# Loads, half scales and tied orders at the head of a two-layer trunk kernel

## The chip, the cores and the metric

The kernel runs on one core of one Trainium2 chip. The core has TensorE (PE in the profile: matrix products and transposes), VectorE (DVE), ScalarE (ACT), GpSimd (POOL) and SyncE (SP, which here issues nearly all transfers between memory and the on-chip buffers). Each engine works through its own list of instructions in order; an instruction waits where its inputs or its buffers are not ready. The metric is the device time of one execution in microseconds (us); the kernel before was timed three times.

## The reference

A sequence of 2048 rows of 1024 numbers goes through two layers, all in 32-bit floats. Only the first products of layer A matter here:

```python
def rms_norm(x, g):
    xf = x.astype(jnp.float32)
    y = xf * lax.rsqrt(jnp.mean(xf * xf, axis=-1, keepdims=True) + EPS)
    return (y * g.astype(jnp.float32)).astype(x.dtype)

def gmlp_mixer(h, w_in, ln_g, ln_b, w_s, b_s, w_out):
    u, v, z = jnp.split(h @ w_in, 3, axis=-1)
    ...

h = rms_norm(x, a_norm_g[i])
x = x + gmlp_mixer(h, a_w_in[i], ...)
```

Layer A normalises each row by its root mean square, scales it by a gain, multiplies by a 1024 x 6144 matrix, mixes in chunks, multiplies by an output matrix and adds. Layer B computes keys and values from the result, attends in bands of nine chunks of 64 rows, multiplies by an output matrix and adds; a last normalisation ends it.

## The kernel before

**Tiling.** The big products use a scheme of seven products in place of eight: rows and columns of the operands are cut in halves, and seven phases, numbered 1, 2, 6, 5, 7, 4, 3 in their order of time, multiply sums and differences of the quarters. The 2048 rows are 16 blocks of 128 rows, taken as eight pairs j = 0 to 7. The even block of a pair is loaded into a tile `ha`, the odd one ("second-row block") into `hb`; of `hb` there are three buffers. A quarter is 128 rows by 512 columns, the first or the second half of a block.

**Precision.** Each operand is a sum of two parts: a rounded one (`hi`, a CAST on ACT) and the difference (`lo`, a TENSOR_TENSOR on DVE). `split`, line 433, makes both. A product is three matrix products, `mm3`, lines 111 to 113: hi x hi, hi x lo of the weights, lo x hi. Lines 434 and 437 are therefore the roundings and the differences, of the weights (tiles `T`, `T_hh`, `T_hl`, 128 x 1024, from raw tiles `rw`) and of the left side (tiles `S`, 128 x 512).

**A block's way.** `block_norm`, line 692, makes four steps: `load` from `x` (line 697, and for block 0 also the gain `gab`), `square` on ACT (line 703), `power` (line 709, a small add on DVE into the tile `ra`, and line 710, the power -1/2 on POOL), `scale` on DVE (line 714), which multiplies the block by its factor and the gain. `s_split`, line 607, then transposes a quarter on PE in four products with the identity (line 611, into a tile `t`, of which there are four buffers), makes `S` hi and lo of it, and stores `S` to memory (`hsd`, line 614) for later passes. There are six `S` buffers. For each pair, `block_c` (line 728) also transposes the second half of `hb` for phase 4 and makes three sums on POOL (lines 734 to 736); `block_d` transposes the first half of `hb`, summed with the second, for phase 5.

**The first 16 steps.** A step is one phase and one pair. In the first 16 (phase 1, then phase 2, pairs 0 to 7 each) the same `S` is multiplied by two groups of weights, number 0 and number 1, 12 products each: 24 products of 128 x 512 per step. Weights of group 0 lie in `T` tiles (eight buffers), those of group 1 in a large tile, `T_hh` in phase 1 and `T_hl` in phase 2. `make_t`, line 448, gives each its `load`, `combine` and `finish` (the split).

**What sets the order.** `run_steps`, line 659, writes the program step by step: the events of a step, its products, then the preparation of the step three later (`LOOK = 3`), then the weights' functions due there. A planner then orders each engine's instructions by what it expects them to cost; a tie (`behind`, `in_order`) puts an instruction after another on its engine. Transfers go into SP's single list in that order. In the program before, the first two `ha` blocks are done by `first_two` (line 927), and ahead of everything PE multiplies zeros 32 times (line 879, tile `wp`).

Of the kernel before, what the change touches and what calls it, by code (L numbers as in the profile page):

```python
# [9 lines left out]
F32 = mybir.dt.float32  # L10
# [23 lines left out]
def trunk_kernel(  # L34
# [349 lines left out]
    with ExitStack() as actx:  # L384
# [43 lines left out]
        def paced(ins):  # L428

            if "evict" in last:  # L430
                behind(ins, last["evict"])

        def split(hi, lo, src, key=None):
            ins = nc.scalar.copy(hi, src)  # L434
            if key:
                in_order(key, ins)
            nc.vector.tensor_tensor(lo, src, hi.bitcast(F32), op=sub)  # L437
            return ins


# [166 lines left out]
        def s_split(ph, j, rows):  # L607

            pt = ptp[0].tile([P, 4, P], F32, tag="t0", name=f"t0_{ph}_{j}", bufs=4)
            for k in range(4):  # L610
                tpose(pt[:, k, :], rows[:, k * P : k * P + P], ident[:])
            t = s_tile(f"S0_{ph}_{j}")
            split(t[:, 0], t[:, 1], pt[:], "S")
            later(1, lambda: paced(nc.sync.dma_start(
                hsd[ph, j][:], t[:].rearrange("p a k c -> p a (k c)").bitcast(F32)
            )))
            return s_views(t)
# [41 lines left out]
        def run_steps(steps, ts, prep, act, events):  # L659


            left = {}
            for s in range(-LOOK, len(steps)):
                for f_ in events.get(s, []):
                    f_()
                if s >= 0:
                    act(s, *steps[s], left.pop(s))
                if s + LOOK < len(steps):
                    left[s + LOOK] = prep(*steps[s + LOOK])
                for f_ in ts.get(s, []):  # L670
                    f_()
# [20 lines left out]
        def block_norm(blk, t):  # L692
# [7 lines left out]

            def square():
                jk = ca.tile([P, D], BF16, tag="acc", name=f"jk{blk}", bufs=25)
                ins = nc.scalar.activation(
                    jk[:], t, AF.Square, scale=1.0 / 32, accum_out=r[:]
                )
                last["square"] = ins.ins.name

            def power():
                nc.vector.tensor_scalar(r[:], r[:], EPS, None, op0=add)
                ins = nc.gpsimd.tensor_tensor(r[:], r[:], mhalf[:], op=ALU.pow)  # L710
                last["power"] = ins.ins.name

            def scale():
                nc.vector.scalar_tensor_tensor(t, t, r[:], gab[:], op0=mul, op1=mul)
# [160 lines left out]
        wz = ca.tile([P, 512], F32R, tag="acc", name="wz", bufs=25)  # L875
        nc.gpsimd.memset(wz[:, 0:256].bitcast(F32), 0.0)
        wp = pmm.tile([P, 512], F32, tag="mm", name="wp")
        for i in range(32):
            mm(wp[:, 0:256], wz[:, 0:P], wz[:, 0:256], start=True, stop=True)
# [13 lines left out]
        for n in range(6):  # L893
            for ph in PH:
# [15 lines left out]
                    offs = ((-5, 1), (-4, 1), (-3, 1))  # L910
                if n == 5 and ph == 3:
                    where = in_big(n, ph, ("hl",))
                add_t(ts, s, n, ph, w_a[n], 2, where, chain_in(n, "hl" if n else "hh"), offs)

        def norm_at(load, s, block, j):
# [8 lines left out]
            ts.setdefault(s, []).append(lambda: todo.pop(0)())  # L924
            at(s + 1, lambda: todo.pop(0)())

        def first_two():
            for fs in zip(block_a(0), block_a(1)):
                for f_ in fs:
                    f_()  # L930
# [1084 lines left out]
```

## Time and profile before

| | |
|---|---|
| three runs | 2649.82, 2651.04, 2652.89 us; median 2651.04 |
| profiled execution | 2655.7 us, its span 2653.6 us |
| mean granted TensorE clock | 0.997 |
| busy in the span | PE 2607.4 us (98%), DVE 1894.2 (71%), ACT 1303.4 (49%), POOL 896.9 (34%) |
| transfers | 718.72 MB, mean 271 GB/s |

The profile is of one execution. Its times count from the span's start. In the rows of the timeline the columns are: start, length, engine, line of the kernel, operation, what it writes and reads, shape, and in brackets the idle time before it with what ended that. A row "x5" merges five that follow each other, and its length runs from the first's start to the last's end. SPq and POOLq are rows of an engine's issuing. Instructions on DVE and ACT overlap a little: the next starts some 0.1 us before the one ahead of it has ended. A row of waits gives the total, the count and the longest. A row of windows gives the stretch, its length, PE's busy time and count, the granted clock of PE (1.00 is full), the busy share of the transfer engines and GB/s.

### The profile page before, as it was taken

Reading aid. Unit: us, or ns where it says so; the run is one execution under the profiler, and the core shown is the slowest. Engines: PE = TensorE matmul, PEld = TensorE weight load, DVE = VectorE, ACT = ScalarE, POOL = GpSimd, SP = SyncE. Lnnn points to the kernel's source line nnn. Section 1 sums busy time; section 2 is a strip of 40 time slices with the busy share of each in tenths; the row PEclk is TensorE's granted clock in tenths of the full one; section 3 lists DMA queues with packets and bytes.
Section 4 is the critical chain, followed back from the end, with each engine's and each line's share of the span. In section 5 each row is a group of like instructions: output and inputs, shape, how many; then the busy total and the mean of one; then the engine's idle time right before and its main releaser. Section 6 shows DMA issues by size and latency. Waiting matters only on the chain. (4 is left out here: it accounts for less than half of the span.)

```text
span 2653.6 us, 37992 instructions
## 1 busy us (share of the span) xinstructions
PE 2607.4 (98%) x12960; PEld 2179.6 (82%) x12960; DVE 1894.2 (71%) x2944; ACT 1303.4 (49%) x2303; POOL 896.9 (34%) x874
## 2 busy tenths in 40 slices
PE   8999999999999999999999999999999999999998
PEld 7888888888888888888877778888887888888886
DVE  5655676866667667757776767778777777877677
ACT  5423243442433434343356466666656655665564
POOL 3611334143152422203234434344332232232245
PEclk9999999999999999999999999999999999999999
DMA  7899998989988869967775587778787666775667
GB/s 286 312 343 333 342 371 321 318 321 345 328 309 301 317 234 323 332 207 270 279 268 193 194 283 228 237 241 267 247 272 254 222 202 221 253 231 162 196 222 253
DMA packets 273856, 718.72 MB, mean 271 GB/s; under 512 B 28800, under 2 KB 68736, under 8 KB 273664
## 3 DMA queue, kind: packets, MB, share of 16 engines
q1 hardware_dynamic: 273664, 716.31, 78.5%
q8 instruction: 103, 1.69, 0.3%
q14 instruction: 89, 0.73, 0.1%
HBM read 531.12 MB, written 174.59 MB: 266 GB/s over the span
## 5 line engine op out<-in xcount | busy, mean ns | idle before, releaser
L111 PE MATMUL P<-T,S 128*128 128x512 f32 x1248 | 496.5, 398 | 2.1 <-ACT S L434 2.1
L112 PE MATMUL P<-T,S 128*128 128x512 f32 x1248 | 488.7, 392 | 0.6 <-DVE T L437 0.6
L113 PE MATMUL P<-T,S 128*128 128x512 f32 x1248 | 489.1, 392 | 0.0
L1437 POOL TENSOR_SCALAR pr<-pr,sl 128x640 f32<-128x640 f32 (+4 forms) x256 | 207.8, 812 | 549.2 <-DVE sl L1436 460.9
L111 PE MATMUL pj<-hh_b,wh_b 128*128 128x512 f32 x768 | 319.4, 416 | 0.9 <-ACT wh_b L228 0.9
L113 PE MATMUL pj<-hh_b,wl_b 128*128 128x512 f32 x768 | 303.9, 396 | 1.5 <-DVE wl_b L229 1.4
L112 PE MATMUL pj<-hl_b,wh_b 128*128 128x512 f32 x768 | 302.4, 394 | 0.1
L1433 ACT ACTIVATE pr<-pr,nm 128x640 f32<-128x640 f32 (+4 forms) x256 | 195.5, 764 | 186.9 <-DVE nm L1426 185.2
L113 PEld LDWEIGHTS P<-T,S 128*128 128x128 f32 x1248 | 235.2, 188 | 50.7
L111 PEld LDWEIGHTS P<-T,S 128*128 128x128 f32 x1248 | 235.6, 189 | 47.1 <-ACT S L434 2.3
L112 PEld LDWEIGHTS P<-T,S 128*128 128x128 f32 x1248 | 235.7, 189 | 45.6 <-DVE T L437 1.0
L1458 DVE TENSOR_TENSOR pt<-tp,pt 128x640 fp32r<-128x640 f32 (+4 forms) x256 | 188.5, 736 | 43.1 <-ACT pt L1457 40.5
L1426 DVE CUSTOM_DVE_ANT_0 pr<-s,bias 128x640 f32<-128x640 f32 (+4 forms) x256 | 188.0, 734 | 32.9 <-PE s L1418 27.0
L1457 ACT CAST pt<-tp 128x640 fp32r<-128x640 f32 (+4 forms) x256 | 158.9, 621 | 52.7 <-PE tp L1453 48.5
L1453 PE MATMUL tp<-ident,pr 128*128 128x128 f32 x1120 | 166.6, 275 | 9.7 <-DVE pt L1458 8.1
L113 PEld LDWEIGHTS pj<-hh_b,wl_b 128*128 128x128 f32 x768 | 144.1, 188 | 36.4 <-DVE wl_b L229 3.9
L1453 PEld LDWEIGHTS tp<-ident,pr 128*128 128x128 f32 x1120 | 130.5, 140 | 44.8 <-issue 16.1
L111 PEld LDWEIGHTS pj<-hh_b,wh_b 128*128 128x128 f32 x768 | 145.0, 189 | 19.0 <-ACT wh_b L228 2.6
L1478 PEld LDWEIGHTS pv<-pt,V 128*128 128x128 f32 x896 | 143.0, 188 | 20.6 <-DVE pt L1458 3.2
L112 PEld LDWEIGHTS pj<-hl_b,wh_b 128*128 128x128 f32 x768 | 145.1, 189 | 16.9 <-DVE hl_b L186 0.6
L1478 PE MATMUL pv<-pt,V 128*128 128x256 f32 (+3 forms) x896 | 154.0, 319 | 2.1 <-ACT pt L1457 1.1
L229 DVE TENSOR_TENSOR wl_b<-raw_b,wh_b 128x1024 fp32r<-128x1024 f32 x96 | 120.1, 1253 | 28.9 <-ACT wh_b L228 27.4
(302 smaller groups left out, 5737.4 us busy)
## 6 DMA issues: line engine op xcount, KB each, us to landing
S<-hsd SPq DMA_DIRECT2D x288, 512.0 KB, 5.5
rw<-in_w_a SPq DMA_DIRECT2D x108, 512.0 KB, 6.5
A<-ytd SPq DMA_DIRECT2D x72, 512.0 KB, 5.4
raw_b<-wk SPq DMA_DIRECT2D x72, 512.0 KB, 4.2
hsd<-S SPq DMA_DIRECT2D x56, 512.0 KB, 4.6
V<-vhd SPq DMA_DIRECT2D x56, 512.0 KB, 5.7
bias<-reld SPq DMA_DIRECT2D x64, 320.0 KB, 3.9
va<-vd SPq DMA_DIRECT2D x32, 512.0 KB, 6.5
```

What stands on the lines that cost most here:

```text
L111: first = mm(ps, lh, rh, start=first, stop=False)
L112: mm(ps, lh, rl, start=False, stop=False)
L113: mm(ps, ll, rh, start=False, stop=last)
L229: tv(wl[:], raw[:], wh[:].bitcast(F32), op=sub)
L1426: nc.vector.tensor_tensor_reduce(out=pr[:, c0:].rearrange("p (a b) -> p a b", a=nseg), in0=ps[:, :nseg, :w], in1=bias[:, c0:].rearrange("p ...
L1433: nc.scalar.activation(pr[:, c0:], pr[:, c0:], AF.Exp, scale=-1.0, bias=nm[:], accum_out=sl[:])
L1437: nc.gpsimd.tensor_scalar(pr[:, c0:], pr[:, c0:], sl[:], 1.0, op0=ALU.mult, op1=ALU.mult)
L1453: ins = tpose(tp[:, b, :], pr[:, b * P : (b + 1) * P], ident[:])
L1457: nc.scalar.copy(oh, tp[:, b0:5, :].rearrange("p a b -> p (a b)"))
L1458: nc.vector.tensor_tensor(pt[:, 2560 + o + b0 * P : 2560 + o + 640], tp[:, b0:5, :].rearrange("p a b -> p (a b)"), oh.bitcast(F32), op=ALU ...
L1478: mm(po[:, q0 * P : q1 * P], vtl[t, p][:, i, hs], rhs, start=(i == blocks[0] and j == 0), stop=(i == 7 and j == 1),)
```

## The change

Five things are done, all in the preparation of the first steps:

1. `opening` replaces `first_two`. Loads go in the order block 0, gain, both weights of group 0, block 1, both weights of group 1. Blocks 0 and 1 are scaled in halves of 512 columns: the first half of each, which phase 1 needs, early, the second halves at the end of the opening.
2. While `begin` is not empty, every instruction that goes through `first` is tied behind the one before it on ACT, and likewise on DVE.
3. 40 zero products instead of 32 come first, and eight more are tied behind block 0's transposes.
4. The weights of phase 2 for both groups are loaded from step 0 on (eight steps ahead of their phase), where they were loaded four to six steps ahead; the steps at which the program writes their split stay the same.
5. The second-row blocks 1 and 2 are loaded one and two steps earlier, that is before the first stores.

```diff
+        def first(eng, ins):
+            if begin:
+                in_order("first " + eng, ins)
+            return ins
...
             for k in range(4):
-                tpose(pt[:, k, :], rows[:, k * P : k * P + P], ident[:])
+                ins = tpose(pt[:, k, :], rows[:, k * P : k * P + P], ident[:])
+            last["tpose"] = ins.ins.name
...
+                if s == -LOOK:
+                    left.update(opening())
                 if s >= 0:
                     act(s, *steps[s], left.pop(s))
-                if s + LOOK < len(steps):
+                if s + LOOK < len(steps) and s + LOOK not in left:
...
-            def scale():
-                nc.vector.scalar_tensor_tensor(t, t, r[:], gab[:], op0=mul, op1=mul)
+            def scale(c=slice(0, D)):
+                first("dve", nc.vector.scalar_tensor_tensor(
+                    t[:, c], t[:, c], r[:], gab[:, c], op0=mul, op1=mul
+                ))
...
-        for i in range(32):
-            mm(wp[:, 0:256], wz[:, 0:P], wz[:, 0:256], start=True, stop=True)
+        def warm(n, after=None):
+            for i in range(n):
+                ins = mm(wp[:, 0:256], wz[:, 0:P], wz[:, 0:256], start=True, stop=True)
+                if after:
+                    behind(ins, after)
+
+        warm(40)
...
+                if n < 2 and ph == 1:
+                    continue
+                if n < 2 and ph == 2:
+                    offs = ((-8, 0), (-5 + n, 1), (-4 + n, 1))
...
-        at(-LOOK, first_two)
+        def opening():
+            begin.append(1)
...
+            load0()
+            for q in range(2):
+                l0(q)
+                c0(q)
+            load1()
+            for q in range(2):
+                l1(q)
+                c1(q)
+            square0()
+            power0()
+            scale0(h0)
+            f0(0)
+            views[0] = prep(*steps[0])
+            warm(8, last["tpose"])
+            f0(1)
+            square1()
+            f1(0)
+            power1()
+            scale1(h0)
+            f1(1)
+            views[1] = prep(*steps[1])
+            scale0(h1)
+            scale1(h1)
+            return views
+
+        at(0, begin.clear)
...
-            norm_at(e - 1, e, block_b, j)
+            norm_at((-1, -1, 0)[j] if j < 3 else e - 1, e, block_b, j)
```

DVE at the very start, rows of the program before (`ra` the factor of a block, `S_1_0` and `S_1_1` the left sides of steps 0 and 1, `T_1` the weights of phase 1, the last number a buffer's):

```order
L714 SCALAR_TENSOR_TENSOR ha_377<-ha_377,ra_378,gab 128x1024
L709 TENSOR_SCALAR ra_380<-ra_380 128x1
L714 SCALAR_TENSOR_TENSOR ha_379<-ha_379,ra_380,gab 128x1024
L437 TENSOR_TENSOR S_1_0_399<-t_1_0_394,S_1_0_399 128x512
L437 TENSOR_TENSOR T_1_01_407<-rw_1_000_402,T_1_00_406 128x1024
L437 TENSOR_TENSOR T_1_11_411<-rw_1_001_404,T_1_10_410 128x1024
L437 TENSOR_TENSOR T_1_hh<-rw_1_000_414,T_1_hh 128x1024
L437 TENSOR_TENSOR S_1_1_448<-t_1_1_443,S_1_1_448 128x512
L437 TENSOR_TENSOR T_1_hh<-rw_1_001_416,T_1_hh 128x1024
L709 TENSOR_SCALAR ra_422<-ra_422 128x1
```

and of the change:

```order
L724 SCALAR_TENSOR_TENSOR ha_385<-ha_385,ra_386,gab 128x512
L444 TENSOR_TENSOR T_1_01_406<-rw_1_000_391,T_1_00_405 128x1024
L444 TENSOR_TENSOR S_1_0_414<-t_1_0_409,S_1_0_414 128x512
L444 TENSOR_TENSOR T_1_11_426<-rw_1_001_393,T_1_10_425 128x1024
L444 TENSOR_TENSOR T_1_hh<-rw_1_000_396,T_1_hh 128x1024
L719 TENSOR_SCALAR ra_388<-ra_388 128x1
L724 SCALAR_TENSOR_TENSOR ha_387<-ha_387,ra_388,gab 128x512
L444 TENSOR_TENSOR T_1_hh<-rw_1_001_398,T_1_hh 128x1024
L444 TENSOR_TENSOR S_1_1_444<-t_1_1_439,S_1_1_444 128x512
L724 SCALAR_TENSOR_TENSOR ha_385<-ha_385,ra_386,gab 128x512
L724 SCALAR_TENSOR_TENSOR ha_387<-ha_387,ra_388,gab 128x512
L719 TENSOR_SCALAR ra_450<-ra_450 128x1
```

The first weight difference stands ahead of `S_1_0`, the second block's add and scale behind three weight differences, and the second halves ahead of the third block's add.

SP after the loads of the first blocks, before (`hsd` the stores of `S`, `rw_2` the weights of phase 2, `hb_640` the third second-row block):

```order
L697 DMA hb_524<-in_x 128x1024
L614 DMA hsd_0_199<-S_1_0_399 128x1024
L614 DMA hsd_1_200<-S_1_1_448 128x1024
L614 DMA hsd_2_201<-S_1_2_466 128x1024
L614 DMA hsd_3_202<-S_1_3_517 128x1024
L614 DMA hsd_4_203<-S_1_4_573 128x1024
L614 DMA hsd_0_223<-S_4_0_589 128x1024
L470 DMA rw_2_100_636<-in_w_a 128x1024
L697 DMA hb_640<-in_x 128x1024
```

and of the change:

```order
L477 DMA rw_2_100_541<-in_w_a 128x1024
L477 DMA rw_2_101_543<-in_w_a 128x1024
L477 DMA rw_2_100_545<-in_w_a 128x1024
L477 DMA rw_2_101_547<-in_w_a 128x1024
L707 DMA hb_553<-in_x 128x1024
L622 DMA hsd_0_199<-S_1_0_414 128x1024
L622 DMA hsd_1_200<-S_1_1_444 128x1024
```

All four weight loads and the block's load have moved ahead of the first store; the other three weight loads stood among later stores.

DVE behind the difference `S_4_0`, before (`T_2` the weights of phase 2, `S_1_5` the left side of step 5, `S_4_1` and `S_5_0` left sides made from second-row blocks):

```order
L437 TENSOR_TENSOR S_4_0_589<-t_4_0_584,S_4_0_589 128x512
L437 TENSOR_TENSOR S_1_5_633<-t_1_5_628,S_1_5_633 128x512
L437 TENSOR_TENSOR S_4_1_650<-t_4_1_645,S_4_1_650 128x512
L437 TENSOR_TENSOR T_2_01_754<-rw_2_100_636,T_2_00_753 128x1024
L437 TENSOR_TENSOR S_1_6_695<-t_1_6_690,S_1_6_695 128x512
L437 TENSOR_TENSOR S_5_0_709<-t_5_0_704,S_5_0_709 128x512
L709 TENSOR_SCALAR ra_641<-ra_641 128x1
L714 SCALAR_TENSOR_TENSOR hb_640<-hb_640,ra_641,gab 128x1024
```

and of the change:

```order
L444 TENSOR_TENSOR S_4_0_618<-t_4_0_613,S_4_0_618 128x512
L444 TENSOR_TENSOR T_2_01_774<-rw_2_100_541,T_2_00_773 128x1024
L444 TENSOR_TENSOR T_2_hl<-rw_2_100_545,T_2_hl 128x1024
L444 TENSOR_TENSOR T_2_11_844<-rw_2_101_543,T_2_10_843 128x1024
L444 TENSOR_TENSOR T_2_hl<-rw_2_101_547,T_2_hl 128x1024
L444 TENSOR_TENSOR S_1_5_662<-t_1_5_657,S_1_5_662 128x512
L719 TENSOR_SCALAR ra_554<-ra_554 128x1
L724 SCALAR_TENSOR_TENSOR hb_553<-hb_553,ra_554,gab 128x1024
L444 TENSOR_TENSOR S_4_1_674<-t_4_1_669,S_4_1_674 128x512
L444 TENSOR_TENSOR S_1_6_719<-t_1_6_714,S_1_6_719 128x512
```

All four weight differences now stand together, ahead of `S_1_5`, of the block's scale, and of `S_4_1` and `S_1_6`.

More of the change, by code (lines that the diff above doesn't have):

```diff
@@ L431, in paced @@
                 behind(ins, last["evict"])
+        begin = []
+        def first(eng, ins):
+            if begin:
+                in_order("first " + eng, ins)
+            return ins
         def split(hi, lo, src, key=None):
-            ins = nc.scalar.copy(hi, src)
+            ins = first("act", nc.scalar.copy(hi, src))
             if key:
                 in_order(key, ins)
-            nc.vector.tensor_tensor(lo, src, hi.bitcast(F32), op=sub)
+            first("dve", nc.vector.tensor_tensor(lo, src, hi.bitcast(F32), op=sub))
             return ins
@@ L925, in norm_at @@
             at(s + 1, lambda: todo.pop(0)())
[L927 to L930, printed above, removed]
-        at(-LOOK, first_two)
+        def opening():
+            begin.append(1)
+            (load0, square0, power0, scale0), (load1, square1, power1, scale1) = (
+                block_a(j) for j in range(2)
+            )
+            tops[0, 1], (l0, c0, f0) = make_t(0, 1, w_a[0], 2, in_t(0, 1), None)
+            tops[1, 1], (l1, c1, f1) = make_t(1, 1, w_a[1], 2, in_big(1, 1, ("hh",)), None)
+            h0, h1 = slice(0, 512), slice(512, D)
+            views = {}
+            load0()
[23 more added lines that the diff above has]
+        at(0, begin.clear)
         for j in range(2, NJ):
```

6 lines of the change are left out of this document (3 added, 3 removed).

## Prediction

> **What bounds the kernel now.** First the busy times and the waits of the first 200 us; the page's share says that TensorE (PE) is the engine whose stream sets the end:
>
> ```profile
> PE 2607.4 (98%) x12960; PEld 2179.6 (82%) x12960; DVE 1894.2 (71%) x2944; ACT 1303.4 (49%) x2303; POOL 896.9 (34%) x874
> ...
> PE t L611 <- DVE hb L714: 3.8, 1, 3.8
> PE P L111 <- ACT S L434: 2.1, 1, 2.1
> ```
>
> Whatever PE idles or runs slowly at the head goes into the total, since nothing later in the order of PE changes. Next PE's own rows, in order of time (start, length, line, operation; idle before it and what ended it), and its granted clock in half microseconds (third number from the end):
>
> ```profile
> 1.26 5.42 PE L879 MATMUL wp<-wz 128*128 128x256 f32 x32 [1.26 <-POOL wz L876]
> 10.68 0.50 PE L111 MATMUL P<-T,S 128*128 128x512 f32 x1 [2.08 <-ACT S L434]
> 20.60 0.39 PE L111 MATMUL P<-T,S 128*128 128x512 f32 x1
> 29.09 0.63 PE L611 MATMUL t<-ident,hb 128*128 128x128 f32 x4 [0.36 <-DVE ra L709]
> 41.08 0.48 PE L111 MATMUL P<-T,S 128*128 128x512 f32 x1
> 46.62 0.60 PE L611 MATMUL t<-ident,ha 128*128 128x128 f32 x4
> 51.47 0.63 PE L611 MATMUL t<-ident,hb 128*128 128x128 f32 x4 [3.82 <-DVE hb L714]
> 51.85 0.57 PE L111 MATMUL P<-T,S 128*128 128x512 f32 x1
> 52.22 0.63 PE L112 MATMUL P<-T,S 128*128 128x512 f32 x1
> 52.65 0.63 PE L113 MATMUL P<-T,S 128*128 128x512 f32 x1
> 59.00 0.60 PE L611 MATMUL t<-ident,ha 128*128 128x128 f32 x4
> ...
> 11.00:11.50 0.50, 0.50 (x3) 0.63 1.01 410
> 17.50:18.00 0.50, 0.50 (x3) 0.54 1.02 410
> 52.00:52.50 0.50, 0.50 (x3) 0.59 1.02 418
> 55.50:56.00 0.50, 0.50 (x3) 0.99 0.95 385
> ```
>
> I count steps from 0: step j of the first eight multiplies a quarter of pair j by the first weights, then by the second ones. Step 1 starts at 20.60, step 4 at 41.08, step 5 at 51.85. Step 4 takes 46.62 - 41.08 = 5.54 us, step 5 takes 59.00 - 51.85 = 7.15: 1.61 us more, at half clock from about 52.1 to 55.5. So two places can give something: the start (half clock 11.1 to 18.0), and the wait of 3.8 us with the 1.6 us behind it. The switches read off these rows, 11.1, 18.0, 52.1 and 55.5, lie 2, 10 and 1 times 3.41 us apart: the clock is decided in stretches of about 3.41 us.
>
> Why the wait:
>
> ```profile
> 18.12 16.95 SPq L614 DMA_DIRECT2D hsd<-S  x5
> 40.49 0.42 SPq L470 DMA_DIRECT2D rw<-in_w_a  x1
> ...
> 45.80 1.05 ACT L434 CAST T<-rw 128x1024 fp32r<-128x1024 f32 x1 [10.12 <-DMA rw<-in_w_a]
> 47.71 1.07 ACT L703 ACTIVATE jk<-hb 128x1024 bf16<-128x1024 f32 x1
> ...
> 50.04 1.28 DVE L714 SCALAR_TENSOR_TENSOR hb<-hb,ra,gab 128x1024 f32<-128x1024 f32 x1 [0.67 <-POOL ra L710]
> ```
>
> SP stands in five stores for 17 us, so the second phase's weights are asked for at 40.49, ScalarE (ACT) sits 10.12 us in its queue until they land at 45.80, and the square of the third second-row block, its scale on VectorE (DVE, to 51.3) and PE's transpose (51.47) follow.
>
> **The change, part by part.** *Loads ahead of the stores.* Four weight loads and the block's load now precede the stores in SP's queue. ACT's 10.12 us and the late square go. The stores move back by five transfers; their readers are the six S buffers, first reused by the rounding of S_1_5, which stands behind the weights in ACT's queue, so I cost that at nothing: transfers follow each other 1.3 us apart (rows of the opening below), which lets the first store land near 31, and that rounding stands near 38. Without these 7 us each late transfer would cost its 1.3. What is late next is DVE's queue, where the four weight differences now stand ahead of S_1_5, the block's scale, S_4_1 and S_1_6. Its prices:
>
> ```profile
> 11.62 2.35 DVE L437 TENSOR_TENSOR T<-rw,T 128x1024 fp32r<-128x1024 f32 x2
> 16.75 0.14 DVE L709 TENSOR_SCALAR ra<-ra 128x1 f32<-128x1 f32 x1
> 17.56 1.28 DVE L714 SCALAR_TENSOR_TENSOR ha<-ha,ra,gab 128x1024 f32<-128x1024 f32 x1 [0.66 <-POOL ra L710]
> 26.79 0.15 DVE L709 TENSOR_SCALAR ra<-ra 128x1 f32<-128x1 f32 x1
> 27.66 1.28 DVE L714 SCALAR_TENSOR_TENSOR hb<-hb,ra,gab 128x1024 f32<-128x1024 f32 x1 [0.73 <-POOL ra L710]
> 31.81 2.31 DVE L714 SCALAR_TENSOR_TENSOR hb<-hb,ra,gab 128x1024 f32<-128x1024 f32 x1 [0.73 <-POOL ra L710]
> 37.18 2.30 DVE L714 SCALAR_TENSOR_TENSOR ha<-ha,ra,gab 128x1024 f32<-128x1024 f32 x1 [2.40 <-POOL ra L710]
> 39.41 1.87 DVE L437 TENSOR_TENSOR S<-t,S 128x512 fp32r<-128x512 f32 x3
> 46.89 1.23 DVE L437 TENSOR_TENSOR T<-rw,T 128x1024 fp32r<-128x1024 f32 x1 [5.60 <-ACT T L434]
> 55.06 2.30 DVE L437 TENSOR_TENSOR T_hl<-rw,T_hl 128x1024 fp32r<-128x1024 f32 x1
> ...
> 37.12 1.29 POOL L734 TENSOR_TENSOR h<-ha,hb 128x512 f32<-128x512 f32 x1
> 38.48 2.16 POOL L735 TENSOR_TENSOR hb<-hb 128x512 f32<-128x512 f32 x1
> 54.13 2.15 POOL L736 TENSOR_TENSOR ha<-hb,ha 128x512 f32<-128x512 f32 x1
> ```
>
> A weight difference costs 1.14 us in a row of two, an S difference 0.60, a scale 1.20 (1.28 with its tail), from the small add to its scale 0.81 to 0.87 because GpSimd's power lies between. A scale or weight difference that meets GpSimd (POOL) takes 2.3, and POOL's 1.29 becomes 2.15.
>
> *The opening.* The first weights take the second block's place in the transfers:
>
> ```profile
> 7.81 1.06 ACT L703 ACTIVATE jk<-ha 128x1024 bf16<-128x1024 f32 x1 [2.28 <-DMA ha<-in_x]
> 9.10 1.04 ACT L434 CAST T<-rw 128x1024 fp32r<-128x1024 f32 x1
> 11.65 1.04 ACT L434 CAST T_hh<-rw 128x1024 fp32r<-128x1024 f32 x1
> 13.08 1.05 ACT L434 CAST T_hh<-rw 128x1024 fp32r<-128x1024 f32 x1
> ```
>
> They land at 7.8 instead of 9.1; the second weights stay at 11.65 and 13.08. I take a scale of half width as 0.68, what an S difference of that width takes. DVE then runs: first weight difference 8.9 to 10.1, S_1_0 to 10.7, next weight difference to 11.9, that of the second weights 12.75 (after their rounding) to 14.0, second block's add 13.9, its half scale 14.7 to 15.4, fourth weight difference to 16.5, S_1_1 (after its transposes) 16.7 to 17.4. PE's first product starts at 9.4 instead of 10.68 and stops for each of these; step 1 starts at 17.7 instead of 20.60: 2.9 us ahead. The 32 warm-up products take 5.42 us; eight more at that mean pace end at 8.0, and the half scale at 7.3, so the first transposes are ready near 8.5, still ahead of ACT, which rounds the weights until 8.8: no cost. Eight at the half-clock pace would end 1.7 us later and cost under 1. The eight products behind the transposes stand in PE's idle time up to 9.4. The ties between first instructions are no work; two scales in halves are two instructions more, inside the sums here.
>
> *What DVE takes back.* It is busy with the opening until 17.4, and the second halves move it to 18.5; in the kernel before it began the third block's add at 16.75. Two adds to 18.9 (the later square ends at 18.8), two scales 19.3 to 21.7, add, S_1_2, add to 22.6, two scales to 25.0, S_1_3 25.6, add, 0.87, the first second-row block's scale 26.4 to 27.7. Before, it began at 27.66: 1.25 ahead, and PE, which reaches that transpose earlier, waits for it. PE resumes at 27.75 instead of 29.09. So of 2.9 us some 1.3 to 1.4 are left. From there to S_4_0 DVE's order and partners are as before: the next scales begin at 30.6 and 35.9 instead of 31.81 and 37.18, S_4_0 ends at 38.85.
>
> *The former wait.* Step 4 runs from 39.7 to 45.2. DVE begins the four weight differences at 38.8. Alone they take 4 x 1.14 = 4.6; meeting the two POOL operations that follow the one of 37.12, pulled ahead by the same 1.25, I add 0.6 and 1.0, nearest the row at 55.06: done at 44.95. Then S_1_5 0.60, add and power 0.85, scale 1.20, S_4_1 and S_1_6 0.60 each: 48.85. Four transpose buffers go round, and the transposes that stand ahead of step 5 need those that S_4_1 and S_1_6 free, so step 5 starts at about 49.3 instead of 51.85: **2.55 us** ahead. Bounds: 47.7 with no meeting at all, 52 with all four at 2.3.
>
> *The clock behind it.* PE then has no product from 45.2 to 49.3, 4.1 us; before it was 5.2 us (46.6 to 51.85), and at the start, from the end of the warm-up at 6.7 to 10.68, 4.0 us; both ended at half clock. A stretch of 3.41 us fits into 4.1 us almost or wholly without products in about half of its possible positions. So the term is 1.6 us (clock stays full) or 0, nearly even; I take 1.6, as the earlier row with 4.0 us lay in one position only.
>
> [...]
>
> *Sum.* 2.55 + 1.6 = 4.2 us. The profiled execution took 2655.7 (span 2653.6 and 2.1 around it), so 2651.5 for one like it; the median of the runs, 2651.04, becomes **2646.8**.
>
> **Rivals.** *The gate closes all the same.* For it: 4.1 us without products against 4.0 that closed it. Against: eight products in the opening and a shorter gap if DVE is quick. Then 2.55 us alone: 2648.5.
>
> *DVE is no bound.* If pairs of adds and scales overlap better than my sum, or POOL's work falls beside the weight differences, step 5 follows step 4 at once: 2.9 at the start, 3.8 and 1.6 at the wait, 8.3 in all, 2642.7; a third of the way from the forecast's 4.2 to that gives about 5.5, 2645.5. For it: DVE stands idle 5.6 us ahead of the row at 46.89. Against: that idle time is what the four differences fill.
>
> *Slower: DVE's queue arrives later than ACT's did.* Place: the four differences. Price: at 2.2 each they end at 47.6; and if the opening runs at half clock, the 16 products before the second block's transposes cost 0.43 each (52.22 to 52.65), 6.9 us from 10.8, and every later DVE row moves by 2.3. Step 5 then starts near 54.2, 2.4 later than before, with the same slow clock: 2653.4. It decides once S_1_6 is done after 51.4. For it: POOL meets DVE in two of the five scales quoted. Against: POOL has only two operations left at that time.
>
> **How the numbers follow.** Forecast 0.38, gate closes 0.32, DVE no bound 0.20, slower 0.10. Range 2643.3 to 2650.8: it takes in the first two with the bounds of DVE's sum (47.7 and 52), most of the third, and leaves the slower case and the ideal outside. A measurement here can tell about 0.2%, 5.3 us, from no change: faster by more, under 2645.7, has the third case and a quarter of the first, 0.30; slower by more, over 2656.3, only the far part of the last, 0.05; within it 0.65.
>
> **What would show it.** Right: ACT's wait of 10.12 us gone; step 1 near 17.7, the first block-b transposes near 27.8 and waiting for DVE's hb; step 5 near 49.3 with PE waiting for an S difference, not for hb; the four T differences in one run on DVE from about 38.8, one or two of them over 1.7 us long. Wrong: step 1 after 19 (clock at half from 11), no PE wait at all between 40 and 50, a store wait on S, or a new wait after 60 us, of which the rows before have none.

## The result

| | before | after |
|---|---|---|
| runs | 11, 2649.82 to 2654.71 us | 11, 2644.72 to 2649.25 us |
| median | 2652.89 us | 2646.22 us |
| ratio, 95% interval | | 0.9974, 0.9967 to 0.9981 |
| profiled execution, its span | 2655.7, 2653.6 us | 2649.25, 2647.5 us |
| granted clock in it | 0.997 | 0.997 |

The change makes the kernel 6.7 us faster (0.26%). The forecast of 2646.8 us is met, but not by its own sum: the sum was 4.2 us, all of it ahead of step 6, and the profile finds 1.8 us there and 4.4 us behind it, where the change moved no instruction. One later execution, the first of the variant with later weight differences, took 3522 us at a mean granted clock of 0.684, and no ratio here includes it.

**The head.** PE's timeline of the changed kernel (start, length, line; idle before it and what ended it), and below it the granted clock in some stretches (third number from the end):

```profile
1.26 6.98 PE L893 MATMUL wp<-wz 128*128 128x256 f32 x40 [1.26 <-POOL wz L888]
17.82 0.39 PE L111 MATMUL P<-T,S 128*128 128x512 f32 x1
28.61 0.63 PE L618 MATMUL t<-ident,hb 128*128 128x128 f32 x4 [0.96 <-DVE ra L719]
40.61 0.48 PE L111 MATMUL P<-T,S 128*128 128x512 f32 x1
46.41 0.66 PE L618 MATMUL t<-ident,ha 128*128 128x128 f32 x4
49.12 1.28 PE L618 MATMUL t<-ident,hb 128*128 128x128 f32 x8 [2.05 <-DVE S L444]
50.05 0.78 PE L111 MATMUL P<-T,S 128*128 128x512 f32 x1
57.19 0.60 PE L618 MATMUL t<-ident,ha 128*128 128x128 f32 x4
...
10.00:14.00 4.00, 3.39 (x13) 2.20 (x13) 3.06 (x5) 3.49 (x5) 0.00 (x0) 1.00 1.03 413
14.00:18.00 4.00, 3.70 (x16) 2.60 (x17) 3.16 (x5) 1.89 (x4) 0.55 (x1) 1.00 1.03 410
50.00:50.50 0.50, 0.50 (x4) 0.50 (x3) 0.50 (x2) 0.37 (x1) 0.50 (x1) 0.52 1.05 401
53.50:54.00 0.50, 0.50 (x3) 0.38 (x3) 0.00 (x0) 0.35 (x1) 0.00 (x0) 1.00 0.82 188
```

The half clock at 11 to 18 us is gone and step 1 starts at 17.82. The wait for `hb` is replaced by one of 2.05 us for an `S` difference. The clock still falls to half at 50.0, for 3.41 us. The transposes that follow step 5 start at 57.19 instead of 59.00: 1.81 us.

DVE's and POOL's timelines of the same kernel:

```profile
22.95 1.52 POOL L720 TENSOR_TENSOR ra<-ra,mhalf 128x1 f32<-128x1 f32 x1 [0.25 <-DVE ra L719]
...
24.51 1.28 DVE L724 SCALAR_TENSOR_TENSOR ha<-ha,ra,gab 128x1024 f32<-128x1024 f32 x1 [0.44 <-POOL ra L720]
27.18 1.28 DVE L724 SCALAR_TENSOR_TENSOR hb<-hb,ra,gab 128x1024 f32<-128x1024 f32 x1 [0.73 <-POOL ra L720]
39.52 1.72 DVE L444 TENSOR_TENSOR T<-rw,T 128x1024 fp32r<-128x1024 f32 x1
41.17 2.31 DVE L444 TENSOR_TENSOR T_hl<-rw,T_hl 128x1024 fp32r<-128x1024 f32 x1
43.41 1.21 DVE L444 TENSOR_TENSOR T<-rw,T 128x1024 fp32r<-128x1024 f32 x1
44.54 1.21 DVE L444 TENSOR_TENSOR T_hl<-rw,T_hl 128x1024 fp32r<-128x1024 f32 x1
47.08 1.28 DVE L724 SCALAR_TENSOR_TENSOR hb<-hb,ra,gab 128x1024 f32<-128x1024 f32 x1 [0.67 <-POOL ra L720]
48.29 3.08 DVE L444 TENSOR_TENSOR S<-t,S 128x512 fp32r<-128x512 f32 x5
```

The four weight differences stand in one row, two of them lengthened (1.72 and 2.31 us) while POOL runs two of its sums (38.00 to 42.40), and `hb`'s scale and the `S` differences wait behind them.

**Far behind.** PE's waits between 1380 and 1420 us (us, times, longest): beside 3.0 us on `Slv` in both kernels, this row in the kernel before, then in the changed one:

```profile
PE vp L111 <- ACT Shv L337: 2.3, 1, 2.3
```

```profile
PE vp L111 <- ACT Shv L337: 0.3, 1, 0.3
```

The same instructions in the same order, with 2.0 us less waiting. The wait of 2.3 us is followed by a half-clock stretch in the kernel before (second window below) and by none in the changed one:

```profile
1405.00:1407.00 2.00, 0.97 (x3) 0.53 (x4) 1.51 (x2) 2.00 (x5) 1.37 (x2) 1.00 1.02 305
1407.00:1409.00 2.00, 2.00 (x6) 1.57 (x6) 2.00 (x3) 1.20 (x3) 2.00 (x2) 0.55 0.92 346
```

What is late there is a store. POOL may change `xo_b` only when its store to `xtd` has landed, and ACT rounds it after POOL. POOL's row in the kernel before and ACT's behind it, then how long that store took to land; then the same for the changed kernel:

```profile
1394.65 1.29 POOL L1222 TENSOR_TENSOR xo_b<-xo_b,xo_b 128x512 f32<-128x512 f32 x1 [8.43 <-DVE Slv L342]
1395.98 0.62 ACT L337 CAST Shv<-xo_b 128x512 fp32r<-128x512 f32 x1 [2.11 <-POOL xo_b L1222]
...
L169 SPq DMA_DIRECT2D xtd<-xo_b x1: 442/442/442, 1387.2 to 1387.2; - x1
...
DMA to landing us min/median/max: 7.3/7.3/7.3
```

```profile
1391.88 1.29 POOL L1273 TENSOR_TENSOR xo_b<-xo_b,xo_b 128x512 f32<-128x512 f32 x1 [6.47 <-DMA xtd<-xo_b]
1393.21 0.62 ACT L337 CAST Shv<-xo_b 128x512 fp32r<-128x512 f32 x1 [0.62 <-POOL xo_b L1273]
...
L169 SPq DMA_DIRECT2D xtd<-xo_b x1: 442/442/442, 1386.9 to 1386.9; - x1
...
DMA to landing us min/median/max: 4.7/4.7/4.7
```

In the kernel before the releaser is put down to DVE, whose difference had long been done; 1387.2 + 7.3 = 1394.5 shows that it was the store. From there the delay goes once round before it meets PE: what ACT does next, the store asked for at 1399.54, the sum that POOL begins at 1403.52 when that store has landed, the rounding on ACT at 1404.84 and PE's product at 1405.51 are each 2.7 to 2.8 us later than in the changed kernel. PE itself was only 0.8 us later at its wait ahead of this (1387.80 against 1387.00); the other 1.9 us are the longer wait. So the questions for the experiments were: is the difference far behind chance of two single profiles, and if not, what in the change reaches so far; and what is each part of the change worth in the head?

### The profile page after: what moved, and what is told of

The parts are those of the page before. It is cut to its first block, busy times and chain, and to the rows that moved or that the text cites. A ratio compares the mean times of both kernels' runs of the same rounds, so it can differ in the third digit from the quotient of the medians.

```text
span 2647.5 us, 38028 instructions
## 1 busy us (share of the span) xinstructions
PE 2607.3 (98%) x12976; PEld 2179.8 (82%) x12976; DVE 1889.1 (71%) x2946; ACT 1303.1 (49%) x2303; POOL 893.7 (34%) x874
```

## The experiments

Theory A: the change gains in the head alone, the rest is chance. Theory B: the order of the loads frees something later. Theory C, formed after the first four runs: the 16 additional products in PE's stream shift something far behind. The "part after step 6" runs from a product of step 6 (62.20 in the kernel before) to PE's last product. The orders of all engines are those of the changed kernel or the kernel before except where said.

**Loads alone.** The kernel before with

```diff
+                if n < 2 and ph == 2:
+                    offs = ((-8, 0), (-5 + n, 1), (-4 + n, 1))
...
-            norm_at(e - 1, e, block_b, j)
+            norm_at((-1, -1, 0)[j] if j < 3 else e - 1, e, block_b, j)
```

> The kernel before, with only the earlier loads (the second phase's weights and the third second-row block ahead of the stores); opening, warm-up and halves as before. Two theories on the 6.7 us that the change gave, of which the profile of the changed kernel shows 1.8 us at step 6 and the rest further on. Theory A (all of the gain is made ahead of step 6; what differs further on is chance of the single profiles): step 1 stays at 20.6, the four weight differences run from 40.0 to 46.2, the scale of the third block ends at 48.8, S_1_6 at 50.0, step 5 starts at 50.5 instead of 51.85 and step 6 at 58.0 (clock half for 3.41 us) or 56.3 (clock full), so 1.3 or 3.0 us faster: ratio 0.9989 to 0.9995. Theory B (the order of the loads also frees something later): more than 4 us faster, ratio under 0.9985, with a step 6 that is only 1.3 us early.

Measured: ratio 0.9990 (0.9981 to 0.9999). Its PE timeline:

```profile
28.92 0.63 PE L611 MATMUL t<-ident,hb 128*128 128x128 f32 x4 [0.36 <-DVE ra L709]
49.42 1.16 PE L611 MATMUL t<-ident,hb 128*128 128x128 f32 x8 [2.05 <-DVE S L437]
55.91 0.60 PE L611 MATMUL t<-ident,ha 128*128 128x128 f32 x4
```

Step 6's transposes are 3.1 us early (59.00 to 55.91), the clock stays full there (step 5's products start 0.23 us apart, at half clock in the kernel before 0.43), as the expectation's better branch had it, and the runs agree with that. Theory B, which asked for more than 4 us, falls: the head is all that the loads need to bring. (In the one profile the part after step 6 is 3.0 us shorter too, 2579.1 against 2582.1; profiles with the same 32 zero products lie between 2579.1 and 2585.3, as the table below shows.)

**Opening alone.** The changed kernel without these two edits.

> The changed kernel with the second phase's weights and the third second-row block back behind the stores; the opening stays. Theory A: step 1 at 17.8, the first second-row transposes at 28.6 and step 4 at 40.6 as in the changed kernel, then the wait for hb is back: weights asked for near 40, ACT waits some 10 us, step 5 at 51.4, half clock behind it, 0.5 us ahead of the kernel before at step 6; time 0.5 us less, ratio 0.9998, no difference that can be measured. Theory B (the opening brings a gain that shows only later): 3 us faster or more, ratio 0.9989 or less.

Measured: 0.9986 (0.9978 to 0.9995), 3.3 us faster, with step 6's transposes at 58.79, 0.2 us early. The gain lies behind the head, and this kernel has 48 zero products.

**32 warm-up products.**

```diff
-        warm(40)
+        warm(32)
...
-            warm(8, last["tpose"])
```

> The changed kernel with 32 warm-up products and without the eight behind the first transposes. The prediction's step: without them the gap up to the first product is 2.8 us instead of 0.7. If the clock then falls to half near 11 us as in the kernel before, the products up to 14.5 take 0.43 instead of 0.23 and step 1 comes at 18.5 to 20; DVE's own queue, 1 us behind PE at the first second-row transposes, hides all but 0.5 of it there: total 0 to 1 us slower, ratio 1.0000 to 1.0004. If the clock stays open: step 1 at 17.8 and no difference. A loss of over 2 us would say that the warm-up carries the gain.

Measured: 0.9986 (0.9977 to 0.9994), 3 us behind the changed kernel's 0.9974, though its head is the same (step 6's transposes at 57.17 and 57.19) and its clock stayed full at the start (products that follow each other stand 0.23 us apart from 11.01 on). That is the loss "over 2 us" of the expectation, but not by the clock: its part after step 6 is 2580.5 us, the changed kernel's 2577.7. By these runs alone it is not certain, since the two intervals overlap (0.9977 to 0.9994 and 0.9967 to 0.9981).

**Weight differences later.** The changed kernel with

```diff
+            last["low"] = low   # in split: the difference just made
...
+            last["S low", ph, j] = last["low"].ins.name   # in s_split
...
+                if n in (0, 1) and ph == 2:   # in make_t, finish
+                    behind(last["low"], last["S low", 1, 6])
```

> The changed kernel with VectorE's four differences of the second phase's weights tied behind S_1_6, so that S_1_5, S_4_1, S_1_6 and the scale of the third second-row block come first. If these differences set step 5 (the prediction's sum, 5 to 6 us of VectorE): the scale runs near 43.0 (GpSimd's power waits for its three sums until 42.4), S_1_6 is done at 46.0, PE's wait of 2.05 us at 49.12 goes, step 5 starts at 47.4 instead of 50.05, the stretch without products is 1.3 us and the clock stays full: step 6 at 53.3 instead of 57.5, 4.3 us faster than the changed kernel, about 2642, ratio to the kernel before 0.996. Rival: the power or the transposes' buffers hold step 5 anyway, and nothing or under 1 us comes of it.

Measured: 0.9959 (0.9945 to 0.9972), over four executions. The same kernel once more, for its waits:

> The changed kernel with the four weight differences behind S_1_6, once more, for a profile of an undisturbed run: scale of the third second-row block near 43.0 behind GpSimd's power, S_1_6 done near 46.0, no PE wait near 49, step 5 near 47.4, clock full from the start to the end; time 2643, ratio 0.996. If step 5 comes later than 48.5 another wait has taken the place.

Measured: 2642.8 us, 0.9958 (0.9945 to 0.9970). Its timelines of DVE and PE:

```profile
42.38 1.28 DVE L729 SCALAR_TENSOR_TENSOR hb<-hb,ra,gab 128x1024 f32<-128x1024 f32 x1 [2.40 <-POOL ra L725]
43.59 1.88 DVE L444 TENSOR_TENSOR S<-t,S 128x512 fp32r<-128x512 f32 x3
45.38 4.35 DVE L444 TENSOR_TENSOR T<-rw,T 128x1024 fp32r<-128x1024 f32 x2
...
46.89 1.04 PE L622 MATMUL t<-ident,hb 128*128 128x128 f32 x8
53.25 0.60 PE L622 MATMUL t<-ident,ha 128*128 128x128 f32 x4
```

The scale and the three `S` differences come first, PE has no wait near 49, the clock stays full (0.999 in the mean), and step 6's transposes start at 53.25: 3.9 us ahead of the changed kernel, of which an estimated 1.6 is the half clock that the changed kernel's profile had at this place. So the four weight differences did set step 5.

**More warm-up in the kernel before.** `range(32)` becomes `range(48)`, nothing else.

> The kernel before with 48 warm-up products instead of 32, nothing else. In the profiles so far the part after step 6 is 2577 to 2578 us long with 48 warm-up products (the changed kernel, the opening alone) and 2579 to 2582 with 32 (before, loads alone, changed kernel with 32), at the same order of work. Theory C (16 more products in PE's stream shift what happens far behind, for instance where its instructions are fetched): step 6 stays within 0.3 us of 59.35, since VectorE sets the first second-row transposes at 29.1 anyway, and the part after it becomes 2 to 4 us shorter: 2650 to 2651, ratio 0.9985 to 0.9992. Theory A (chance, or the head alone): no difference, ratio within 0.0005 of 1, and the profile's waits near 1405, 2004 and 2177 come as they do in the kernel before.

Measured: 0.9981 (0.9972 to 0.9990), 5 us faster for 16 zero products. The head gains 1.3 us, where the expectation allowed 0.3: step 6's transposes at 57.70, since the clock, at half for 3.41 instead of 6.83 us at the start, lets PE and with it DVE run earlier:

```profile
28.11 0.63 PE L611 MATMUL t<-ident,hb 128*128 128x128 f32 x4 [0.34 <-DVE ra L709]
50.29 1.08 PE L611 MATMUL t<-ident,hb 128*128 128x128 f32 x4 [3.60 <-DVE hb L714]
57.70 0.60 PE L611 MATMUL t<-ident,ha 128*128 128x128 f32 x4
```

The part after step 6 is 2576.4 instead of 2582.1 us. Theory A, that the head is all and the rest chance, falls.

**The changed kernel again.**

> The changed kernel once more, on the same chip as the others of this group. Ratio 0.9974 as before if its gain does not depend on the chip or the hour; 0.9985, as the variant with 32 warm-up products had it, if the difference between those two was chance. The profile's part after step 6: 2577 to 2578 us by theory C, anything from 2577 to 2582 by chance.

Measured: 0.9973 (0.9963 to 0.9982), so the gain came again. The part after step 6, 2572.7 us, is under the 2577 to 2578 that theory C gave: a single profile of the same kernel can differ by 5 us here. Of that, 1.8 us lie near 1586, where the first profile of the changed kernel (2577.7) had another 3.41 us of half clock.

**Weight differences later, 32 warm-up products.**

> The same with 32 warm-up products and without the eight behind the first transposes. Its head is that of the run with 48 (the clock stayed full at the start with 32 in the changed kernel). Theory C: the part after step 6 is 2 to 4 us longer than with 48, 2645 to 2647. Theory A: the same time within 1 us, 2643.

Measured: 2648.85 us, 0.9982 (0.9973 to 0.9990), 6 us slower than with 48 on the same chip; step 6's transposes at 53.55 against 53.25; part after step 6 2585.3. Theory C again, by more than it asked; the profile has a stretch of half clock near 1588 in it.

**What the additional products move.** The page of the changed kernel has this queue of the kind "instruction" (queue, packets, MB, share):

```profile
q8 instruction: 104, 1.70, 0.3%
```

1.70 MB in 104 packets is 16384 bytes each, and the trace has 26598 rows of PE (25952 products and weight loads, 646 others), 256 per packet; in the kernel before it is 103 packets for 26566 rows. By these counts I take the packets to carry PE's instructions. A zero product is two of the rows, so if so, 16 of them shift every later packet by 32 instructions against the program. Three more kernels test the place of the packets, not their number.

*16 products 40 us later.* The variant with 32 warm-up products, and in PE's gap ahead of step 5 (the planner moves a few rows of the other engines in the first phases with it)

```diff
+        def fill():
+            wq = pmm.tile([P, 512], F32, tag="mm", name="wq")
+            for i in range(16):
+                ins = mm(wq[:, 0:256], wz[:, 0:P], wz[:, 0:256], start=True, stop=True)
+                behind(ins, last["tpose", 1, 7])
+
+        at(5, fill)
```

> The variant with 32 warm-up products, and 16 zero products of the same size put into PE's gap ahead of step 5 (behind the transposes of S_1_7): 48 zero products in all, the last 16 of them 40 us later than in the changed kernel. Theory C (their number shifts where PE's instructions are fetched further on; in the profiles with 32 a fetch starts 1.6 to 1.8 us after the store of xo_b that GpSimd waits for near 1390, and that store lands after 7.1 to 7.3 us; with 48 the fetch is over before the store is asked for, and it lands within 5.1 to 5.7): the longest landing of the stores to xtd between 1365 and 1410 is 5.1 to 5.7 again, the part after step 6 is 2573 to 2578 us instead of 2580.5, ratio 0.997 or less. Rival (the warm-up at the start matters in itself): landing 7.2, part after step 6 2580, ratio 0.998 at best. Clock: with products in the gap no half-clock stretch near 50 to 53, step 6 at 56.0 instead of 57.5; if the products themselves delay the transposes, step 5 comes up to 0.5 later than 50.05.

Measured: 0.9968 (0.9955 to 0.9981); part after step 6 2577.0; that store lands in 5.3 us. (The store that POOL waits for is the one asked for at 1387.2, not the next one, which the expectation measures from.) PE's gap:

```profile
47.35 2.16 PE L985 MATMUL wq<-wz 128*128 128x256 f32 x16
49.64 1.16 PE L618 MATMUL t<-ident,hb 128*128 128x128 f32 x8
56.13 0.60 PE L618 MATMUL t<-ident,ha 128*128 128x128 f32 x4
```

With products in the gap the clock did not fall here (step 5's products from 50.87 on start 0.23 us apart), and step 6's transposes start 1.06 us earlier than in the changed kernel, though the products delay the transposes by 0.5.

*One whole packet more.* The kernel before with 160 warm-up products of 64 columns.

> The kernel before with 160 warm-up products of a quarter of the size instead of 32 (128 more, or 256 instructions with their weight loads, which is one fetch of PE's queue: 16384 bytes, one about every 256 instructions). Theory C by position: the fetches fall where they fell with 32, the longest landing of the stores to xtd near 1390 is 7 us again and the part after step 6 is 2579 to 2585. Rival (more products are better in themselves): 5.1 to 5.7, and 2573 to 2578. The warm-up is up to 2 us longer, so the time itself says little: 2651 to 2656.

Measured: 1.0085, 2676 us. The narrow products do not take a quarter of the time (last section), the warm-up lasts to 35.6 us, and the planner moves rows of the first phases; so the time says nothing. The part after step 6 does: 2583.4 us, and the store lands in 7.0 us again. With 128 more products the packets fall where they fell with 32.

*An eighth of a packet further.* The variant with later weight differences and `warm(24)`, then 32 products of 128 columns, in place of `warm(40)`: 64 in all (here too a few rows of the first phases move).

> The variant with the weight differences behind S_1_6, with 64 zero products instead of 48 in about the same time (32 of them half as wide): the fetches move on by another eighth of their distance. Head as with 48: step 6 at 53.6. Theory C says only that the part after step 6 changes with the place of the fetches: the fetch near 1390 comes 3 to 6 us earlier still and stays clear of the stores, landing 5.1 to 5.7; the other waits may come or go by 1 us each, so 2640 to 2646. By chance alone: 2643.

Measured: 0.9965 (0.9952 to 0.9979); the store lands in 5.7 us. Its packet came only 0.9 us earlier against the store than with 48 products, not the 3 to 6 us expected. The part after step 6 is 2578.7: 3 us of waits near 1275 and 1293 have come, which the run of the same group with 16 products in the gap also shows and which stay unexplained.

Thirteen profiles together (of the variant with later differences the second); start of the packet against the time at which the store was asked for, landing of that store, both in us (from the trace's packets and the store's rows), PE's excess over the shortest passage in any of these profiles at two places (with the half clock behind the first), and the part after step 6:

```
zero products      packet - store   landing   near 1405   near 1539   part after step 6
32  before              +5.3          7.3        3.6         1.1          2582.1
32  loads alone         +5.2          7.2        3.5         1.6          2579.1
32  changed, 32         +5.1          7.1        1.9         1.5          2580.5
32  later diff., 32     +5.2          7.2        3.6         1.6          2585.3
160 before, narrow      +5.0          7.0        1.9         1.1          2583.4
48  changed             -1.5          4.7        0.1         0.0          2577.7
48  changed again       -1.5          4.5        0.1         0.0          2572.7
48  opening alone       -0.2          5.7        0.6         0.0          2576.9
48  before, 48          -1.5          5.2        0.3         0.0          2576.4
48  later diff.         -1.4          5.2        0.4         0.0          2575.2
48  16 in the gap       -1.4          5.3        0.4         0.0          2577.0
48  no opening          -1.5          4.5        0.3         0.0          2574.1
64  later diff., 64     -2.3          5.7        0.6         0.0          2578.7
```

A packet that starts 5.0 to 5.3 us behind the store's request falls into the store's last pieces, and the store lands after 7.0 to 7.3 us; one that starts ahead of it leaves 4.5 to 5.7. This holds in all 13 profiles, with the products added at the start, 40 us later, or by a whole packet, so the wait near 1405 goes with the place of the packet, not with the number of products. The traces say more. They have sixteen landings for each such store: in the five slow ones, fifteen have come after 5.5 to 5.9 us and the last, alone, 1.3 to 1.8 us behind them; in the other eight the last is within 0.3 us of the one before it. So the packet goes with one piece of sixteen that is held up, and POOL waits for that piece. Why a packet of 0.93 to 0.96 us costs more than its own time is not shown. What else sets the landing, the other fifteen pieces, is as late in two of the eight (opening alone and 64, 5.6 and 5.7 us) and up to 1.2 us earlier in the rest.

The wait near 1539 is of the same kind. PE waits there for a load of `Qh`. In the five profiles with 32 or 160, a packet starts 2.9 to 3.2 us after that load was asked for, fifteen of its landings have come after 5.6 to 6.1 us, the last comes at 7.7 to 8.4, and PE waits 0.5 to 1.2 us. In the other eight no packet starts in that time, the load lands in 5.4 to 6.2 us, and PE does not wait. One delay of 0.8 to 1.0 us near 1529, where PE waits for a rounding on ACT, goes the other way.

The means of the last column are 2582.1 us (five with 32 or 160) and 2575.7 (seven with 48). Of these 6.4 us, the two waits with their packets account for 2.6 and 1.4, and the one near 1529 takes 0.9 back; the rest, of which the largest parts lie near 1995 and 2170 (0.9 and 0.8 us), was not traced.

**Without the opening.** The kernel before with the loads, the later weight differences, and 48 warm-up products in one row.

> The kernel before with three edits alone: the loads ahead of the stores, the four weight differences behind S_1_6, and 48 warm-up products in one row; the old opening stays (no halves, no first weights ahead of the second block, no ties, no products behind the transposes). If VectorE's row of scales sets the head, as the waits at the first second-row transposes say, the opening is worth nothing here: step 1 at 19.5 to 20.5 instead of 17.8, but the scale of the first second-row block near 27.5, S_4_0 done near 39.9, step 5 at 47.3 to 47.8, step 6 at 53.5 to 54.0, as with the opening; the store to xtd lands within 5.1 to 5.8; ratio 0.9955 to 0.9970 (with the opening it was 0.9958). If the opening is worth what it puts step 1 ahead: step 6 at 55 to 56, ratio 0.9970 to 0.9980.

Measured: 2641.46 us, 0.9957 (0.9944 to 0.9971), as fast as with the opening. PE's timeline:

```profile
18.21 0.39 PE L111 MATMUL P<-T,S 128*128 128x512 f32 x1
27.77 0.63 PE L613 MATMUL t<-ident,hb 128*128 128x128 f32 x4 [0.52 <-DVE ra L712]
45.73 1.04 PE L613 MATMUL t<-ident,hb 128*128 128x128 f32 x8
52.10 0.60 PE L613 MATMUL t<-ident,ha 128*128 128x128 f32 x4
```

Step 1 starts at 18.21 and step 6's transposes at 52.10, 1.3 and 1.4 us ahead of the expected ranges. The first second-row transposes start at 27.77, with the opening at 28.91 (later differences) and 28.61 (changed kernel). The halves, the first weights ahead of the second block and the ties are worth nothing that shows in the time (0.9957 without, 0.9958 with them), and cost 0.8 to 1.1 us at this place. What stays open is whether they keep the clock at the start more often: with the opening and 48 or 64 zero products it was full there in five of five profiles, with the old one and 48 in one of two.

## Why the prediction was right or wrong

**The opening.** Step 1 came at 17.82 (forecast 17.7) and the clock stayed full. *What DVE takes back* failed in two ways. The size: PE resumed at 28.61, not 27.75, 0.5 and not 1.3 us ahead, since POOL's power met a DVE scale at 22.95 and took 1.52 instead of 0.55 us, which the sum of adds and scales did not have. And the owner: the gain at this place is the clock's. 48 products in the old opening give 28.11 with 3.41 us of half clock left, 27.77 with none (the last run); the new opening does worse.

**Loads ahead of the stores.** Right: ACT's wait of 10.12 us is gone, the four differences stand in one row (39.52 to 45.75, forecast 38.8 to 44.95), meeting POOL cost 0.6 and 1.2 us (forecast 0.6 and 1.0), and PE waits for an `S` difference. Step 5 came at 50.05 instead of 49.3, 0.7 of it the delay brought along from the opening (`S_4_0` done at 39.52, not 38.85): 1.8 us of the 2.55.

**The clock term.** "1.6 us or 0, nearly even; I take 1.6." In both profiles of the changed kernel the clock fell at 50; of its 22 timed runs 10 have a share of 0.999, and the profile with a single fall ahead of the end has 0.998. So the record speaks for nearly even, as far as these shares tell, and taking 1.6 as the whole was too much; a mean over the runs gets about half of it. That is also what the rival "the gate closes all the same" (its name for this fall to half clock) said for the profile. The loads alone kept the clock through a like gap (last product at 46.21, next at 50.34; in the changed kernel 45.92 and 50.05), so gap length alone does not decide. Position fits, as the prediction supposed: from the first record of full clock on, the traces have its changes whole multiples of 3.41 us apart (in the kernel before at 4.31, 11.13, 17.96, 52.09, 55.51, 1407.18 and 1410.60: 2, 2, 10, 1, 396 and 1 times). In the changed kernel one such stretch, 46.61 to 50.02, lies wholly between two products (one ends at 46.31, the next starts at 50.05), and 1.4 us of transposes in it did not hold the clock; in all six profiles in which it fell at this gap, the stretch has 0.5 us of products at most. In the loads alone the two that meet the gap, 44.80 to 48.22 and 48.22 to 51.63, have 1.8 and 1.3 us of products. How much is enough stays open: at the start a stretch with 1.9 us of products still closed it (later differences with 32) and one with 1.2 did not (no opening). So does whether transposes count for less.

**The sum.** The step that failed is the sentence under the first fence, that what PE idles at the head goes into the total and nothing later changes because PE's order does not. The order behind the first steps did not change, the place of the instruction packets did, and the waits near 1405 and 1539 with it. The sum priced the eight and eight zero products as time in idle gaps, at nothing; they bring some 3 to 6 us (32 against 48 products: 3 in the changed kernel by the ratios, 6 with later differences, 5 in the kernel before, 1.3 of it in the head). The head gives 1.8 us with the clock at half, an estimated 3.4 without (step 5's 1.61 added). That 2646.8 fell so near to 2646.22 is luck, two errors that cancel: 4.2 instead of 6.7 us, taken from a median of 2651.04 over three runs that was 2652.89 over eleven.

**The rivals.** *DVE is no bound* did not happen, and the later differences show what it would have been worth: 3.9 us at step 6. *DVE's queue arrives later than ACT's* did not happen; two of its four meetings did.

**The signs.** A store wait on `S` did come, against the forecast:

```profile
53.65 0.59 ACT L441 CAST S<-t 128x512 fp32r<-128x512 f32 x1 [3.28 <-DMA hsd<-S]
```

PE had none behind it, so it cost nothing. A new wait after 60 us, the other such sign, came too: 0.72 us for ACT at 1526 (near 1529 in the time of the kernel before), which none of the profiles with 32 has. The forecast looked for new waits only, and not for old ones that could shrink.

## What to carry to other kernels

A wait far behind an edit can change though no order there does (here a wait of 2.3 us became 0.3): where a profile shows stores whose landing decides, find the instruction packets beside them (here with 1.3 to 1.8 us on one piece of a store), and shift them by a few zero products before believing in a gain of a few microseconds. Test the parts of a change one by one with the number of PE's instructions kept; here the loads and 16 zero products carry the gain, and the most elaborate part, the opening, none that could be measured. Ahead of a full row on DVE, put first what PE's next transposes need: moving four differences behind three small ones gave 4.0 us more in the time, the loads that brought them forward 2.7.

## What was not expected of the hardware

- A store of 512 KB landed in 7.0 to 7.3 us in each of the five profiles in which an instruction packet of 16384 bytes met it, and in 4.5 to 5.7 in the others; 1.3 to 1.8 us of this are one held-up piece of sixteen.
- Narrow zero products did not run faster here. 160 of them with 64 columns lasted 34.34 us, 0.215 each, with a median weight load of 333 ns; those with 256 columns start 0.213 us apart in the kernel before as long as their loads take 330 ns, up to 4.2 us, and 0.12 apart after that, with a median load of 192 ns and 283 ns for the product:

```profile
L879 PEld LDWEIGHTS wp<-wz x160: 285/333/333, 1.3 to 35.1; 128*128 128x128 f32 x160
L879 PE MATMUL wp<-wz x160: 401/401/419, 1.3 to 35.2; 128*128 128x64 f32 x160
```

```profile
L879 PEld LDWEIGHTS wp<-wz x32: 187/192/333, 1.3 to 6.3; 128*128 128x128 f32 x32
L879 PE MATMUL wp<-wz x32: 278/283/582, 1.3 to 6.4; 128*128 128x256 f32 x32
```

  The rows of the granted clock say 1.00 for both, but the trace has no record of the clock ahead of a first one, of full clock: at 38.4 us with the narrow products, at 4.2 to 7.3 us in the other twelve of the thirteen profiles. In each, the last load of 330 ns or more ends within 0.2 us of it. So 34 us of products of 64 columns brought no record of full clock, and 3 to 6 us of zero products that began with 256 columns did.
- 48 warm-up products do not keep the clock for certain: with them it fell at 12.45 us in the kernel before, and with 32 it stayed full in the changed kernel with 32.
